# A projection on other PSUM banks, and one table of angles built later

## The chip, the cores and the metric

The kernel runs on one core of one Trainium2 chip. The metric is the device time in microseconds of one execution; lower is better. Three runs of the kernel before gave a median of 1317.6 us (1317.01 to 1318.38). The profile used here is of one further execution, which took 1318.57 us.

The engines named are PE (matrix products), PEld (its weight loads), DVE (the vector engine), ACT (activations and copies), POOL and SP (the queue that issues the large loads). PSUM is the memory that PE writes its products to; here it is cut into eight banks of 128 x 512 numbers.

## The reference

One decoder layer on 256 tokens of width 1024, in float32. The normalised input is multiplied by one wide matrix, and four branches take their parts of the result:

```
proj = h @ w_in
att  = dsa_attention(...)      # indexer relu(q_idx . k_idx), top-64 keys, latent attention
cnv  = short_conv(...)         # gated convolution of width 3
ssm  = s5_mixer(...)           # diagonal complex state space, scan over time, then a gate
mem_o = memory_attention(...)  # 4 heads into 256 memory tokens
merged = sum_r sigmoid(gate_r) * (branch_r @ w_branch[r])
h = layer_norm(alpha * h + merged @ w_o)
h = layer_norm(alpha * h + moe(h))     # 32 experts, top 4 of each token
```

In `s5_mixer` the decay of a state over a step is `exp(lam * dt)`, so the powers of it that a chunked scan needs are sines and cosines of multiples of an angle. `u` is the scan's input, `h @ w_in` in the columns of the state space.

## The kernel before

The program is written as one main stream of projections (`main`, L957 on) and three streams beside it, which are traced a step at a time between the projections: the scan (`scan_all`), the indexer and sparse attention (`sparse_all`) and the memory attention (`memory_all`). After tracing, a scheduler reorders instructions of an engine, except those given to `keep_in_program_order`. Each engine then runs its own list strictly in that order, so an instruction that waits holds up all that stands behind it on its engine.

**Weights.** SP loads each weight matrix in pieces of 1 MB into slabs. A weight is then split into a high and a low part: ACT casts it (L320), DVE subtracts (L325, 128x1024 at a time, two per piece), and PE makes three products of them (L386 to L388). The splits are traced some weights ahead of their use.

**PSUM.** Three pools of banks: `P` with four, `PT` (transposes) with two and `PD` (small products) with two. A product waits until what its bank held before has been read. The projections' results (`pu` for the scan's input, `pmq` for the memory's queries, `pq` for the sparse queries, `pcv` for the convolution) all come from `P`, as do the indexer's scores `prl` (read by ACT's relu, L825) and the latents `pckv` (read by DVE, L1046).

**The scan.** `scan_tables` (L548 on) makes tables of angles. L581 makes the angles within a chunk (`sn`, 128x288), L584 those between chunks (`js`, 128x1024); `wrap` (L569 to L573) brings an angle into the range of the sine. ACT takes the sines (L594 to L597), and DVE goes on (L598 to L651). `scan_in` turns the scan's input round, and `scan_part(m)`, for four quarters m, first builds two matrices on DVE (L679 to L686, eight instructions, of which six of 128x1024), multiplies them on PE (`pkt`, L696/L697, and the transposes `pe`, L707), sends one through DRAM, and then runs the scan itself: `pV` on PE (L719), its copy on ACT (L722), turns by `js` and `jc` on DVE (L660 to L669 and L724 to L730) and the products `py`. `pkt` and `pV` stand in `PD`, as do the logits `pml` of the memory attention (L923), which DVE reduces (L926, L927) and ACT exponentiates (L929).

**After the branches.** Gates (`pg`), branch outputs (`pbr`), the output product and the router follow, and then the experts: a stream of 1 MB loads of their weights which starts when the slabs of the part ahead come free.

Of the kernel before, what the change touches and what calls it, by code (L numbers as in the profile page):

```python
# [17 lines left out]
AF = mybir.ActivationFunctionType  # L18
OP = mybir.AluOpType
# [10 lines left out]
NG, GN, GP = 32, 16, 64  # L30
SC = 8
NJ = T // SC
# [139 lines left out]
def tile_trunk(ctx, tc, a, out):  # L172
    nc = tc.nc
    PE, V, S, G = nc.tensor, nc.vector, nc.scalar, nc.gpsimd
# [16 lines left out]
    def P(nm):  # L191
        return ps.tile([128, 512], FT, name=nm, tag="pp", bufs=4)
# [261 lines left out]
    def small(shape, nm, bufs=2):  # L454
        return keep.tile(shape, FT, name=nm, bufs=bufs)
# [71 lines left out]
    p = PT("pvc")  # L527
# [25 lines left out]
    res = {}  # L553

    def scan_tables():

        L = B(128, 2, NG)
        p = PT("pl")
# [9 lines left out]
        def wrap(t, kt):  # L568
            V.tensor_scalar(kt, t, 1.0 / TWO_PI, MAGIC, op0=OP.mult, op1=OP.add)  # L569
            V.tensor_scalar(kt, kt, MAGIC, None, op0=OP.subtract)  # L570
            for c in (PI_A, PI_B, PI_C):
                V.scalar_tensor_tensor(t, kt, -c, t, op0=OP.mult, op1=OP.add)
            V.tensor_scalar(t, t, PI_IN, -PI_IN, op0=OP.min, op1=OP.max)  # L573
# [3 lines left out]
        kk, jj = B(128, NG * NJ), B(128, NG, NJ)  # L577
        G.iota(jj.ap, pattern=[[0, NG], [1, NJ]], base=0, channel_multiplier=0, allow_small_or_imprecise_dtypes=True)
        wrap(XA.ap[:, 1, :], kk.ap[:, :NG])
        sn, js, jc = sn_, js_, jc_  # L580
        V.tensor_tensor(sn.ap, tau.ap, XA.ap[:, 1:2, :].to_broadcast([128, NT, NG]), op=OP.mult)  # L581
        wrap(sn.ap, kk.ap[:, :NT * NG].rearrange("p (t g) -> p t g", t=NT))
        yield
        V.tensor_tensor(js.ap, jj.ap, sn.ap[:, SC, :].unsqueeze(2).to_broadcast([128, NG, NJ]), op=OP.mult)  # L584
        wrap(js.ap, kk.ap.rearrange("p (g j) -> p g j", g=NG))
        kk.free()
        jj.free()
        yield
        mag, th = mag_, B(128, NG)
        V.tensor_tensor(mag.ap, tau.ap, XA.ap[:, 0:1, :].to_broadcast([128, NT, NG]), op=OP.mult)  # L590
# [2 lines left out]
        sh = B(128, NT, NG)  # L593
        S.activation(sh.ap, sn.ap, AF.Sin, scale=0.5)  # L594
        S.activation(sn.ap, sn.ap, AF.Sin)
        S.activation(jc.ap, js.ap, AF.Sin, scale=0.5)
        S.activation(js.ap, js.ap, AF.Sin)  # L597
        V.tensor_tensor(jc.ap, jc.ap, jc.ap, op=OP.mult)  # L598
        V.tensor_scalar(jc.ap, jc.ap, -2.0, 1.0, op0=OP.mult, op1=OP.add)
        yield  # L600
        V.tensor_tensor(sh.ap, sh.ap, sh.ap, op=OP.mult)
        pr = pr_
        V.tensor_scalar(pr.ap, sh.ap, -2.0, 1.0, op0=OP.mult, op1=OP.add)
# [6 lines left out]
        pi = sn  # L610
# [18 lines left out]
        for i in range(2):  # L629
            p = PT("pc")  # L630
# [18 lines left out]
        pis, npr = pis_, tau  # L649
# [4 lines left out]
        res.update(pr=pr, pi=pi, pis=pis, npr=npr, js=js, jc=jc, mag=mag)  # L654
        yield

    def turn(dst, src, sine, sign):

        lo, hi = slice(0, 64), slice(64, 128)
        V.scalar_tensor_tensor(dst[lo], src[hi], sign, sine[hi], op0=OP.mult, op1=OP.mult)  # L660
        V.scalar_tensor_tensor(dst[hi], src[lo], -sign, sine[lo], op0=OP.mult, op1=OP.mult)

    def scan_part(m):

        pr, pi, pis, npr, js, jc, mag = (res[k].ap for k in ("pr", "pi", "pis", "npr", "js", "jc", "mag"))
        gs = slice(m * 8, m * 8 + 8)
        b1f = bb1.ap.rearrange("p g n -> p (g n)")[:, m * 128:]
        b1, b2, C1, C2 = bb1.ap[:, gs], bb2.ap[:, gs], CC[0].ap[:, gs], CC[1].ap[:, gs]
        tg = lambda t, k: t[:, k:k + SC, gs].rearrange("p t g -> p g t").unsqueeze(3).to_broadcast([128, 8, SC, GN])  # L669
        bg = lambda t: t.unsqueeze(2).to_broadcast([128, 8, SC, GN])  # L670

        blk1, blk2 = B(128, SLAB), B(128, SLAB)
        Cp, tE = carve(blk1, *[(128, 8, SC, GN)] * 2)
        M3 = carve(blk1, (128, 1024), (128, 8, 128))[1]
        kp = carve(blk1, (128, 1024), (128, 2, (2 * SC - 1) * GN))[1]
        E, M1 = carve(blk2, (128, 8, SC, GN), (128, 8, 128))
        Vs, Vr, rt, a8 = carve(blk2, *[(128, 8 * NJ)] * 3, (128, 8, NJ))
        C0, St = res["io2"][1 + m % 2 * 2:3 + m % 2 * 2]
        V.tensor_copy(C0.ap[0:64], C1[0:64])  # L679
        V.tensor_scalar(C0.ap[64:128], C1[64:128], -1.0, None, op0=OP.mult)  # L680
        V.tensor_tensor(Cp.ap, bg(C1), tg(npr, 1), op=OP.mult)
        V.tensor_tensor(tE.ap, bg(C2), tg(pi, 1), op=OP.mult)
        V.tensor_tensor(Cp.ap, Cp.ap, tE.ap, op=OP.subtract)
        V.tensor_tensor(E.ap, bg(b1), tg(pr, 0), op=OP.mult)
        V.tensor_tensor(tE.ap, bg(b2), tg(pis, 0), op=OP.mult)
        V.tensor_tensor(E.ap, E.ap, tE.ap, op=OP.add)  # L686
        yield

# [3 lines left out]
        p = PD("pkt")  # L692
# [11 lines left out]
        for q4 in range(2):  # L704
            p = PT("pe")
# [11 lines left out]
        p = PD("pV")  # L717
# [18 lines left out]
        p = PD("py")  # L736
# [16 lines left out]
    def scan_in():  # L753

        uP = res["uP"]
        W1, U = B(128, 8, SC, GN), res["U"]
        for s4 in range(2):
            p = PT("pus")
            for i in range(4):
                PE.transpose(p[:, i * 128:(i + 1) * 128],  # L760
                             uP.ap[:, SC - 1 - (s4 * 4 + i)].rearrange("p m j -> p (m j)"), ident)
            S.copy(W1.ap[:, :, s4 * 4:s4 * 4 + 4, :].rearrange("p q s n -> p s q n"),
                   p.rearrange("p (s q n) -> p s q n", s=4, q=8))
        for q4 in range(2):
            p = PT("puq")
            for i in range(4):
                PE.transpose(p[:, i * 128:(i + 1) * 128],
                             W1.ap[:, q4 * 4 + i].rearrange("p s n -> p (s n)"), ident)
            S.copy(U.ap[:, q4 * 4:q4 * 4 + 4].rearrange("p q m j -> p (q m j)"), p)
        W1.free()  # L770
        res["Y1"] = res["io2"][0]
        yield
# [180 lines left out]
        res["br3"] = oX  # L953


    def projs(ids, xx, nm, put):
        for c, i in enumerate(ids):  # L957
            p = P(nm)
            for j in range(2):
                w = take(i, j)  # L960
                projT(p[:, j * 256:(j + 1) * 256], w, 0, xx)
                w.done()
            put(c, p)
            yield
# [4 lines left out]
    def main():  # L969
# [6 lines left out]
        for c, i in enumerate(ID_V):  # L976
            w = take(i)
            p = P("pv")
# [25 lines left out]
        p = P("pqi")  # L1004
# [9 lines left out]
        p = P("pki")  # L1014
# [14 lines left out]
        wix = keep.tile([128, 2, IH], FT, name="wix")  # L1029
# [28 lines left out]
        res.update(io_blk=io_blk, U=U, io2=carve(io_blk[1], (128, SC, 8, GN), *[(128, 8, GN), (128, 8, NJ + 1)] * 2))  # L1058
        for c, _ in enumerate(projs(ID_S, hX, "pu", lambda c, p: S.copy(
                uP.ap[:, :, 2 * c:2 * c + 2, :].rearrange("p s m j -> p m j s"),  # L1060
                p.rearrange("p (m j s) -> p m j s", m=2, s=SC)))):
            if c == 0:
                latents()
            yield
# [11 lines left out]
        for c2 in range(2):  # L1076
# [11 lines left out]
            for i in range(2):  # L1088
                c = c2 * 2 + i
                V.tensor_scalar(cv.ap[:, i, :], vv.ap[:, i, 0:T], cw(c, 0), cw(c, 3), op0=OP.mult,  # L1090
                                op1=OP.add)
                for k in (1, 2):
                    V.scalar_tensor_tensor(cv.ap[:, i, :], vv.ap[:, i, k:k + T], cw(c, k), cv.ap[:, i, :],
                                           op0=OP.mult, op1=OP.add)
# [8 lines left out]
        for n, r in enumerate((1, 3, 2, 0)):  # L1103
            if r == 2:
# [3 lines left out]
                for c in range(4):  # L1108
                    w = take(ID_GL, c // 2)
                    p = P("pgl")  # L1110
# [15 lines left out]
            for d2 in range(KC // 2):  # L1126
                p = P("pg")
# [7 lines left out]
                p = P("pbr")  # L1135
# [3 lines left out]
                m = mg.ap[:, 2 * d2:2 * d2 + 2, :].rearrange("p a t -> p (a t)")  # L1139
# [78 lines left out]
    def both(*gens):  # L1218
        live = list(gens)
        while live:  # L1220
            for g in list(live):
                try:
                    next(g)
                except StopIteration:
                    live.remove(g)
            yield

    def scan_all():
        for _ in range(SCAN_AT):
            yield  # L1230
        yield from scan_tables()
        while "uP" not in res:
            yield
        yield from scan_in()
        yield from both(scan_part(0), scan_part(1))
        yield from both(scan_part(2), scan_part(3))
        yield from scan_out()
# [83 lines left out]
    for b in range(2):  # L1321
        mu, r, nm = mv1[:, b, 0:1], r1[:, b:b + 1], nm1[:, b:b + 1]
# [15 lines left out]
        p = PD("prk")  # L1338
# [434 lines left out]
```

## Time and profile before

| | us |
|---|---|
| median of three runs | 1317.6 (1317.01 to 1318.38) |
| the profiled execution | 1318.57 |
| its span (first to last instruction) | 1316.7 |
| PE busy | 1214.9 (92%) |
| DVE busy | 469.8 (36%) |
| ACT busy | 319.6 (24%) |
| mean DMA rate over the span | 352 GB/s |

A group of rows names an engine, a line of the kernel, the operation, the tile written and the tile read. Buffer numbers are left out, so two buffers of one name look alike. The number in brackets at a row's end is how long the engine stood idle ahead of the instruction, and which instruction ended that. The instructions of an engine overlap a little, so that a run of matmuls of 0.28 us each can start every 0.12 us. PEclk is the share of full speed that PE's clock was granted.

### The profile page before, as it was taken

How to read it: one execution, taken by the hardware profiler on the slowest of the kernel's cores; microseconds unless marked ns; L12 is line 12 of the kernel's file. 1: busy time of each engine (PE TensorE's matmuls, PEld its weight loads, DVE VectorE, ACT ScalarE, POOL GpSimd, SP SyncE). 2: the span in 40 equal slices, each digit the busy share in tenths (PEclk: the TensorE clock that was granted, in tenths of full speed). 3: DMA queues.
4: the chain of work that ended last, by engine and by line, in shares of the span. 5: the costliest groups of instructions: out<-in, count | busy, mean ns of one | idle time of the engine just before them, and what ended most of it. 6: DMA issues, size and time to landing. Idle time of an engine off the chain costs nothing. (4 is left out here: it accounts for less than half of the span.)

```text
span 1316.7 us, 17368 instructions
## 1 busy us (share of the span) xinstructions
PE 1214.9 (92%) x6928; PEld 669.2 (51%) x6928; DVE 469.8 (36%) x972; ACT 319.6 (24%) x639; POOL 107.3 (8%) x158
## 2 busy tenths in 40 slices
PE   8799999999999999999999999898989898899984
PEld 8699999889853333333343333333333333333321
DVE  5896976755632133221212213021221212130214
ACT  4735545544422111011211102011010102020101
POOL 1103020246110000000000000000000000000001
PEclk9999999999999999999999999999999999999998
DMA  9816458974889999999999999999999999999993
GB/s 249 273 36 172 130 144 291 292 249 164 319 324 412 419 420 419 419 420 419 420 419 418 420 419 421 420 419 420 419 421 418 420 420 418 421 419 420 412 413 131
DMA packets 115238, 463.38 MB, mean 352 GB/s; under 512 B 19304, under 2 KB 54192, under 8 KB 68016
## 3 DMA queue, kind: packets, MB, share of 16 engines
q1 hardware_dynamic: 112512, 456.37, 87.6%
q0 software_dynamic: 2608, 5.83, 1.7%
q8 instruction: 57, 0.93, 0.3%
q14 instruction: 29, 0.24, 0.0%
q10 hardware_dynamic: 32, 0.01, 0.0%
HBM read 459.09 MB, written 3.08 MB: 351 GB/s over the span
## 5 line engine op out<-in xcount | busy, mean ns | idle before, releaser
L1500 PE MATMUL hp<-slab,slab 128*64 128x512 f32 x2048 | 484.7, 597 | 31.2 <-DMA slab<-in_w_up_dram 30.8
L1500 PEld LDWEIGHTS hp<-slab,slab 128*64 128x64 f32 x2048 | 157.6, 137 | 321.5 <-issue 238.5
L1518 PE MATMUL dp<-slab,slab 128*64 128x512 f32 x1024 | 232.3, 597 | 2.2 <-ACT slab L1515 1.2
L1518 PEld LDWEIGHTS dp<-slab,slab 128*64 128x64 f32 x1024 | 72.4, 137 | 127.3 <-issue 120.9
L325 DVE TENSOR_TENSOR slab<-slab,slab 128x1024 fp32r<-128x1024 f32 (+1 forms) x90 | 110.3, 1235 | 55.8 <-ACT slab L320 50.5
L320 ACT CAST slab<-slab 128x1024 fp32r<-128x1024 f32 x90 | 92.6, 1048 | 78.9 <-DMA slab<-in_w_in_dram 16.5
L1391 ACT ACTIVATE slab<-pxs,pcol 128x128 f32<-128x128 f32 x128 | 48.0, 457 | 235.2 <-PE pxs L1386 225.1
L1491 DVE CAST slab<-id 128x64 fp32r<-128x64 f32 x34 | 5.1, 192 | 221.3 <-PE hp L1494 212.5
L1377 POOL TENSOR_SCALAR slab<-slot_i,slot 128x64 f32<-128x64 f32 x32 | 13.9, 453 | 803.6 <-PE pta L1513 701.6
L388 PE MATMUL pg<-slab,slab 128*128 128x256 f32 x256 | 74.4, 291 | 0.0
L386 PE MATMUL pg<-slab,slab 128*128 128x256 f32 x256 | 74.3, 290 | 0.0
L387 PE MATMUL pg<-slab,slab 128*128 128x256 f32 x256 | 73.6, 288 | 0.0
L1386 PEld LDWEIGHTS pxs<-slab,slab 128*128 128x128 f32 x512 | 59.7, 192 | 25.7 <-issue 23.5
L1457 ACT CAST slab<-psg 128x256 fp32r<-128x256 f32 x16 | 6.0, 372 | 255.5 <-PE psg L1455 255.5
L1386 PE MATMUL pxs<-slab,slab 128*128 128x128 f32 x512 | 65.9, 282 | 1.1 <-DVE slab L1377 0.7
L1443 DVE TENSOR_SCALAR slab<-hp 128x256 f32<-128x256 f32 x64 | 27.0, 422 | 76.5 <-PE pta L1513 76.5
L1534 DVE TENSOR_TENSOR slab<-slab,psc 128x512 f32<-128x512 f32 x60 | 38.6, 684 | 43.7 <-PE psc L1530 43.7
L386 PEld LDWEIGHTS pg<-slab,slab 128*128 128x128 f32 x256 | 49.8, 194 | 2.0 <-issue 1.5
L388 PEld LDWEIGHTS pg<-slab,slab 128*128 128x128 f32 x256 | 49.9, 195 | 1.1 <-issue 1.1
L387 PEld LDWEIGHTS pg<-slab,slab 128*128 128x128 f32 x256 | 49.8, 194 | 0.3 <-issue 0.2
L1513 PE MATMUL pta<-ident,slab 128*128 128x128 f32 x128 | 26.5, 290 | 24.2 <-ACT slab L1515 24.0
L1515 ACT COPY slab<-pta 128x256 f32<-128x256 f32 x64 | 23.9, 375 | 94.3 <-PE pta L1513 94.3
(446 smaller groups left out, 1533.8 us busy)
## 6 DMA issues: line engine op xcount, KB each, us to landing
slab<-in_w_up_dram SPq DMA_DIRECT2D x256, 1024.0 KB, 19.9
slab<-in_w_down_dram SPq DMA_DIRECT2D x126, 1024.0 KB, 19.9
slab<-in_w_in_dram SPq DMA_DIRECT2D x29, 1024.0 KB, 6.6
slab<-in_w_branch_dram SPq DMA_DIRECT2D x8, 1024.0 KB, 7.3
slab<-in_w_mem_kv_dram SPq DMA_DIRECT2D x4, 1024.0 KB, 10.9
slab<-in_w_o_dram SPq DMA_DIRECT2D x4, 1024.0 KB, 8.1
slab<-kp_d POOLq DMA_DIRECT2D x32, 64.0 KB, 3.9
slab<-in_w_down_dram SPq DMA_DIRECT2D x4, 512.0 KB, 16.6
```

The costliest lines, as they stand in the source:

```text
L320: ins = S.copy(r_(hi[:, sl]), src[:, sl])
L325: ins = eng.tensor_tensor(r_(lo[:, p0:p1]), src[:, p0:p1], hi[:, p0:p1], op=OP.subtract)
L386: PE.matmul(dst, lh, rh, start=first, stop=False)
L387: PE.matmul(dst, lh, rl, start=False, stop=False)
L388: PE.matmul(dst, ll, rh, start=False, stop=last)
L1386: PE.matmul(p[:, i * 128:(i + 1) * 128], hN.ap[:, b, k * 128:(k + 1) * 128], self.S2.ap[:, b].rearrange("p e s -> p (e s)"), start=b == 0 ...
L1391: S.activation(self.xs.ap[:, k, :], p[:, i * 128:(i + 1) * 128], AF.Identity, bias=col(3, k), scale=col(2, k))
L1443: V.tensor_scalar(l.ap, hv[:, :, :, 1], LIMIT, -LIMIT, op0=OP.min, op1=OP.max)
L1500: PE.matmul(hp[nb][e * 64:(e + 1) * 64, :], xs[:, k, e * CAP:(e + 1) * CAP], w, start=start, stop=k == KC - 1, skip_group_check=True)
L1513: PE.transpose(p[:, j * 128:(j + 1) * 128], l.ap[:, j, :], ident)
L1518: PE.matmul(dp[nb][e * 64:(e + 1) * 64, :], aT.ap[:, k, e * 64:(e + 1) * 64], w, start=k == 0, stop=k == KC - 1, skip_group_check=True)
L1534: V.tensor_tensor(y, y, p, op=OP.add)
```

## The change

1. `projs` takes the pool of banks as an argument, and the scan's input is projected with `PD` in place of `P`.
2. The angles between chunks leave `scan_tables`: their product, their wrap, their two sines and the two instructions that make the cosine move into a new stream `turns`, traced after `scan_in`. A copy of 128x32 (`step8`) keeps the angles they are made from.
3. `scan_tables` now waits, while it is traced, until the indexer's weights `wix` are there, before the instructions after the sines.
4. For the first two quarters of the scan, six of the eight instructions that build the two matrices are given to `keep_in_program_order`.

```diff
--- before.py
+++ after.py
@@ -580,11 +580,8 @@
         sn, js, jc = sn_, js_, jc_
         V.tensor_tensor(sn.ap, tau.ap, XA.ap[:, 1:2, :].to_broadcast([128, NT, NG]), op=OP.mult)
         wrap(sn.ap, kk.ap[:, :NT * NG].rearrange("p (t g) -> p t g", t=NT))
-        yield
-        V.tensor_tensor(js.ap, jj.ap, sn.ap[:, SC, :].unsqueeze(2).to_broadcast([128, NG, NJ]), op=OP.mult)
-        wrap(js.ap, kk.ap.rearrange("p (g j) -> p g j", g=NG))
-        kk.free()
-        jj.free()
+        step8 = small([128, NG], "step8", 1)
+        V.tensor_copy(step8, sn.ap[:, SC, :])
         yield
         mag, th = mag_, B(128, NG)
         V.tensor_tensor(mag.ap, tau.ap, XA.ap[:, 0:1, :].to_broadcast([128, NT, NG]), op=OP.mult)
@@ -593,11 +590,9 @@
         sh = B(128, NT, NG)
         S.activation(sh.ap, sn.ap, AF.Sin, scale=0.5)
         S.activation(sn.ap, sn.ap, AF.Sin)
-        S.activation(jc.ap, js.ap, AF.Sin, scale=0.5)
-        S.activation(js.ap, js.ap, AF.Sin)
-        V.tensor_tensor(jc.ap, jc.ap, jc.ap, op=OP.mult)
-        V.tensor_scalar(jc.ap, jc.ap, -2.0, 1.0, op0=OP.mult, op1=OP.add)
         yield
+        while "wix" not in res:
+            yield
         V.tensor_tensor(sh.ap, sh.ap, sh.ap, op=OP.mult)
         pr = pr_
         V.tensor_scalar(pr.ap, sh.ap, -2.0, 1.0, op0=OP.mult, op1=OP.add)
@@ -654,6 +649,19 @@
         res.update(pr=pr, pi=pi, pis=pis, npr=npr, js=js, jc=jc, mag=mag)
         yield
 
+        def turns():
+
+            V.tensor_tensor(js.ap, jj.ap, step8.unsqueeze(2).to_broadcast([128, NG, NJ]), op=OP.mult)
+            wrap(js.ap, kk.ap.rearrange("p (g j) -> p g j", g=NG))
+            kk.free()
+            jj.free()
+            yield
+            S.activation(jc.ap, js.ap, AF.Sin, scale=0.5)
+            S.activation(js.ap, js.ap, AF.Sin)
+            V.tensor_tensor(jc.ap, jc.ap, jc.ap, op=OP.mult)
+            V.tensor_scalar(jc.ap, jc.ap, -2.0, 1.0, op0=OP.mult, op1=OP.add)
+        res["turns"] = turns
+
     def turn(dst, src, sine, sign):
 
         lo, hi = slice(0, 64), slice(64, 128)
@@ -676,13 +684,15 @@
         E, M1 = carve(blk2, (128, 8, SC, GN), (128, 8, 128))
         Vs, Vr, rt, a8 = carve(blk2, *[(128, 8 * NJ)] * 3, (128, 8, NJ))
         C0, St = res["io2"][1 + m % 2 * 2:3 + m % 2 * 2]
-        V.tensor_copy(C0.ap[0:64], C1[0:64])
-        V.tensor_scalar(C0.ap[64:128], C1[64:128], -1.0, None, op0=OP.mult)
-        V.tensor_tensor(Cp.ap, bg(C1), tg(npr, 1), op=OP.mult)
-        V.tensor_tensor(tE.ap, bg(C2), tg(pi, 1), op=OP.mult)
+
+        hold = tc.keep_in_program_order if m < 2 else lambda ins: ins
+        hold(V.tensor_copy(C0.ap[0:64], C1[0:64]))
+        hold(V.tensor_scalar(C0.ap[64:128], C1[64:128], -1.0, None, op0=OP.mult))
+        hold(V.tensor_tensor(Cp.ap, bg(C1), tg(npr, 1), op=OP.mult))
+        hold(V.tensor_tensor(tE.ap, bg(C2), tg(pi, 1), op=OP.mult))
         V.tensor_tensor(Cp.ap, Cp.ap, tE.ap, op=OP.subtract)
-        V.tensor_tensor(E.ap, bg(b1), tg(pr, 0), op=OP.mult)
-        V.tensor_tensor(tE.ap, bg(b2), tg(pis, 0), op=OP.mult)
+        hold(V.tensor_tensor(E.ap, bg(b1), tg(pr, 0), op=OP.mult))
+        hold(V.tensor_tensor(tE.ap, bg(b2), tg(pis, 0), op=OP.mult))
         V.tensor_tensor(E.ap, E.ap, tE.ap, op=OP.add)
         yield
 
@@ -953,9 +963,9 @@
         res["br3"] = oX
 
 
-    def projs(ids, xx, nm, put):
+    def projs(ids, xx, nm, put, bank=P):
         for c, i in enumerate(ids):
-            p = P(nm)
+            p = bank(nm)
             for j in range(2):
                 w = take(i, j)
                 projT(p[:, j * 256:(j + 1) * 256], w, 0, xx)
@@ -1058,7 +1068,7 @@
         res.update(io_blk=io_blk, U=U, io2=carve(io_blk[1], (128, SC, 8, GN), *[(128, 8, GN), (128, 8, NJ + 1)] * 2))
         for c, _ in enumerate(projs(ID_S, hX, "pu", lambda c, p: S.copy(
                 uP.ap[:, :, 2 * c:2 * c + 2, :].rearrange("p s m j -> p m j s"),
-                p.rearrange("p (m j s) -> p m j s", m=2, s=SC)))):
+                p.rearrange("p (m j s) -> p m j s", m=2, s=SC)), PD)):
             if c == 0:
                 latents()
             yield
@@ -1232,6 +1242,7 @@
         while "uP" not in res:
             yield
         yield from scan_in()
+        yield from res["turns"]()
         yield from both(scan_part(0), scan_part(1))
         yield from both(scan_part(2), scan_part(3))
         yield from scan_out()
```

In the built programs the counts on the engines stay as they are but for one more DVE instruction (the copy) and one more load of an activation table on ACT. The instructions below carry the number of the slab that they use.

On ACT, from the scan's tables to the relu of the second pair of indexer scores (`prl`). Before, with the sines of the angles between chunks at L596 and L597:

```order
L1037 COPY wix<-pckv 128x8
L1038 ACTIVATE slab_608,ss<-pckv 128x128
L596 ACTIVATE slab_121<-slab_121 128x1024
L1037 COPY wix<-pckv 128x8
L1038 ACTIVATE slab_608,ss<-pckv 128x128
L597 ACTIVATE slab_121<-slab_121 128x1024
L1039 ACT_TABLE_LOAD
L1039 ACTIVATE rr<-ss,eps_t 128x2
L634 COPY slab_123<-pc 128x512 x2
L825 ACTIVATE slab_124<-prl 128x128
```

After (the lines have other numbers there: the same sines are L659 and L660, the relu is L835):

```order
L1049 ACT_TABLE_LOAD
L1049 ACTIVATE rr<-ss,eps_t 128x2
L629 COPY slab_123<-pc 128x512 x2
L835 ACTIVATE slab_124<-prl 128x128
L835 ACTIVATE slab_683<-prl 128x128
L835 ACTIVATE slab_124<-prl 128x128
L835 ACTIVATE slab_683<-prl 128x128
L320 CAST slab_927<-slab_517 128x1024
L659 ACT_TABLE_LOAD
L659 ACTIVATE slab_121<-slab_121 128x1024
L1069 COPY slab_694<-pu 128x64x8
L1062 COPY slab_612<-pct 128x256
```

The first sine stands behind the first four relus and a table load of its own, and no longer ahead of them; the second stands later still.

On PE, where the first query projection `pq` ends, with the scan's first products `pkt` and `pe` and the memory's logits `pml`. Before, the end of the second `pkt`, then `pe`, `pml` and the second `pq`:

```order
L696 MATMUL pkt<-slab_704,slab_122 32x16
L697 MATMUL pkt<-slab_1001,slab_122 32x112
L696 MATMUL pkt<-slab_704,slab_122 32x16
L697 MATMUL pkt<-slab_1001,slab_122 32x112
L707 MATMUL pe<-ident,slab_1002 128x128 x8
L923 MATMUL pml<-slab_198,slab_124 128x256 x4
L386 MATMUL pq<-slab_196,slab_1018 128x256
L387 MATMUL pq<-slab_197,slab_1018 128x256
```

After, the end of the first `pq`, then `pml` and the second `pq`:

```order
L386 MATMUL pq<-slab_196,slab_927 128x256
L387 MATMUL pq<-slab_197,slab_927 128x256
L388 MATMUL pq<-slab_196,slab_928 128x256
L933 MATMUL pml<-slab_198,slab_527 128x256 x4
L386 MATMUL pq<-slab_196,slab_996 128x256
L387 MATMUL pq<-slab_197,slab_996 128x256
L388 MATMUL pq<-slab_196,slab_997 128x256
```

And after, where the second `pq` (48 matmuls) ends:

```order
L386 MATMUL pq<-slab_196,slab_996 128x256
L387 MATMUL pq<-slab_197,slab_996 128x256
L388 MATMUL pq<-slab_196,slab_997 128x256
L706 MATMUL pkt<-slab_695,slab_122 32x16
L707 MATMUL pkt<-slab_1057,slab_122 32x112
L706 MATMUL pkt<-slab_695,slab_122 32x16
```

The two pairs `pkt` and `pe` came ahead of `pml` and now come behind it and behind the second `pq`. All three of `pml`, its twin and `pkt` write banks of `PD`, so `pkt` now waits until the exponentials of `pml` are read out; the built program's first `pkt` waits for the second exponential.

On DVE, ahead of the reduction of `pml` (L926 before, L936 after; L686 and L696 are the last instruction of a quarter's matrices, MAX and MATCH_REPLACE are the rounds of the indexer's top-k). Before, the end of the second quarter's matrices:

```order
L685 TENSOR_TENSOR slab_1001<-slab_123,slab_122 128x1024
L840 MAX m_1011<-slab_608 128x8
L686 TENSOR_TENSOR slab_1002<-slab_1002,slab_1001 128x1024
L841 MATCH_REPLACE slab_608<-m_1011,slab_608 128x128
L325 TENSOR_TENSOR slab_1019<-slab_517,slab_1018 128x1024
L840 MAX m_1014<-slab_608 128x8
L325 TENSOR_TENSOR slab_1019<-slab_517,slab_1018 128x1024
L841 MATCH_REPLACE slab_608<-m_1014,slab_608 128x128
L325 TENSOR_TENSOR slab_1191<-slab_1073,slab_1190 128x1024
L840 MAX m_1157<-slab_608 128x8
```

After, the same place:

```order
L695 TENSOR_TENSOR slab_1067<-slab_123,slab_122 128x1024
L851 MATCH_REPLACE slab_527<-m_1077,slab_527 128x128
L696 TENSOR_TENSOR slab_1068<-slab_1068,slab_1067 128x1024
L850 MAX m_1080<-slab_527 128x8
L936 TENSOR_REDUCE mx<-pml 128x2
L851 MATCH_REPLACE slab_527<-m_1080,slab_527 128x128
L937 TENSOR_SCALAR mx<-mx 128x2
L936 TENSOR_REDUCE mx<-pml 128x2
L325 TENSOR_TENSOR slab_1111<-slab_1051,slab_1110 128x1024
```

The reduction stood 20 rows behind the second quarter's L686; it now stands two rows behind it, and ahead of that L686 stand two more splits of a weight and more of the rounds.

## Rows read from the trace of the kernel before

**Rows 1.** The profile page: slices of a fortieth of the span, 32.9 us each
```profile
DVE  5896976755632133221212213021221212130214
...
DMA  9816458974889999999999999999999999999993
GB/s 249 273 36 172 130 144 291 292 249 164 319 324 412 419 420 419 419 420 419 420 419 418 420 419 421 420 419 420 419 421 418 420 420 418 421 419 420 412 413 131
```

**Rows 2.** PE's waits, 55 to 200 us: in total, times, longest
```profile
PE pu L386 <- ACT slab L825: 7.1, 1, 7.1
PE pe L707 <- DVE slab L686: 1.4, 1, 1.4
```

**Rows 3.** PE's timeline, 57 to 75 us: start, duration, line, operation, [idle before]
```profile
57.88 0.71 PE L820 MATMUL prl<-slab 32*128 32x128 f32 x8
65.72 0.58 PE L386 MATMUL pu<-slab,slab 128*128 128x256 f32 x1 [7.13 <-ACT slab L825]
...
69.29 0.28 PE L387 MATMUL pu<-slab,slab 128*128 128x256 f32 x1
```

**Rows 4.** ACT's timeline, 60 to 66 us
```profile
60.43 1.06 ACT L596 ACTIVATE slab<-slab 128x1024 f32<-128x1024 f32 x1 [3.64 <-DVE slab L573]
...
62.78 1.28 ACT L1039 ACT_TABLE_LOAD   x1
...
65.21 0.79 ACT L825 ACTIVATE slab<-prl 128x128 f32<-128x128 f32 x4
```

**Rows 5.** DVE's timeline, 52 to 75 us
```profile
52.09 1.23 DVE L584 TENSOR_TENSOR slab<-slab,slab 128x1024 f32<-128x1024 f32 x1
...
74.27 1.23 DVE L325 TENSOR_TENSOR slab<-slab,slab 128x1024 fp32r<-128x1024 f32 x1 [0.82 <-ACT slab L320]
```

**Rows 6.** Windows: length, busy time of five engines, PEclk, DMA share, GB/s
```profile
66.00:68.00 2.00, 2.00 (x10) 2.00 (x11) 2.00 (x5) 0.00 (x1) 0.00 (x0) 0.50 0.00 0
168.00:170.00 2.00, 2.00 (x12) 2.00 (x12) 2.00 (x5) 1.19 (x2) 0.27 (x1) 0.56 0.35 54
120.00:178.00 58.00, 55.83 (x523) 52.01 (x522) 56.84 (x108) 28.64 (x56) 9.93 (x22) 0.97 0.44 125
```

**Rows 7.** DVE's timeline, 92 to 105 us
```profile
92.99 1.21 DVE L686 TENSOR_TENSOR slab<-slab,slab 128x1024 f32<-128x1024 f32 x1
...
94.38 1.22 DVE L325 TENSOR_TENSOR slab<-slab,slab 128x1024 fp32r<-128x1024 f32 x1
...
100.36 0.28 DVE L841 MATCH_REPLACE8 slab<-m,slab 128x128 f32<-128x128 f32 x1
...
103.68 0.69 DVE L926 TENSOR_REDUCE mx<-pml 128x2 f32<-128x512 f32 x1 [0.57 <-PE pml L923]
```

**Rows 8.** ACT's timeline, 104 to 108 us
```profile
104.65 1.28 ACT L929 ACT_TABLE_LOAD   x1 [1.20 <-DVE mx L927]
105.95 0.47 ACT L929 ACTIVATE slab<-pml,mx 128x256 f32<-128x256 f32 x1
...
106.77 0.20 ACT L929 ACTIVATION_READ_ACCUMULATOR slab<-pml,mx 128x1 f32 x1
```

**Rows 9.** PE's timeline, 99 to 113 us
```profile
102.61 1.89 PE L923 MATMUL pml<-slab,slab 128*128 128x256 f32 x8
104.15 0.47 PE L386 MATMUL pq<-slab,slab 128*128 128x256 f32 x1
...
110.09 1.87 PE L719 MATMUL pV<-slab,slab 128*128 128x32 f32 x16
...
112.62 0.36 PE L386 MATMUL pcv<-slab,slab 128*128 128x256 f32 x1
```

**Rows 10.** ACT's timeline, 119 to 121 us
```profile
119.52 0.36 ACT L722 COPY slab<-pV 128x256 f32<-128x256 f32 x1
```

**Rows 11.** DVE's timeline, 120 to 180 us
```profile
120.89 0.42 DVE L660 SCALAR_TENSOR_TENSOR slab<-slab,slab 64x256 f32<-64x256 f32 x1
...
177.35 1.23 DVE L325 TENSOR_TENSOR slab<-slab,slab 128x1024 fp32r<-128x1024 f32 x1
```

## Prediction

> **What bounds the kernel now.** I read the page's slices first. From the thirteenth on, about 395 us into the span, the core moves 412 to 421 GB/s and its DMA share is 9 almost to the end: the experts are bound by their weight loads [rows 1]. Ahead of that the rates go up and down between 36 and 324 GB/s, so the first 360 us or so are bound by the engines. The experts' loads follow the slabs that this part frees, so what it gains or loses moves the end one for one.
>
> Second, the waits of PE. Between 55 and 200 us two matter: 7.1 us of the scan's input `pu` for ACT's relu, and 1.4 us of a transpose `pe` for DVE [rows 2]. On the timeline PE ends the indexer's scores at 58.59 (57.88 + 0.71) and starts `pu` at 65.72 [rows 3].
>
> Third, why the relu is late. ACT stands idle 3.64 us until DVE has wrapped the angles between chunks, then takes two sines, loads a table for 1.28 us, and reaches the relu only at 65.21 [rows 4]. `pu` does not use what the relu writes: it needs one of the four banks of its pool, all held by scores and latents.
>
> Fourth, the clock. After the wait PE runs at 0.50 of its speed, the 1.2 GHz level [rows 6]: 16 matmuls take 3.57 us, from 65.72 to 69.29 [rows 3]. At the full level, 2.4 GHz, 48 take 5.94 us, from 104.15 to 110.09, or 0.124 each [rows 9].
>
> Last, DVE. From 120 to 178 us it is busy 56.84 of 58 us, and PE 55.83 [rows 6]: there PE has little slack against DVE, and a lead on PE alone need not pass through.
>
> **Other banks for `pu`.** Nothing writes the two banks of the small products between the start of the program and the memory's logits, so `pu` can start right after the scores, at about 59.0 (I add 0.4 to 58.59, since a copy on ACT that PE needs ahead of it now stands behind two sines). That takes away 7.13 - 0.4 = 6.7 us of waiting and 3.57 - 16 x 0.124 = 1.6 us of slow clock, 8.3 us in all. The second `pu` has a bank of its own and waits for nothing new.
>
> **The angles between chunks.** On DVE nothing is taken away: their product and wrap still stand at the same place in its list, from 52.09 on [rows 5], and one small copy is added (0.2 us). On ACT the sines move behind the first four relus, with a table load of their own. These relus write a buffer that DVE's tables use before; from 52.1 I count 27 instructions of DVE up to the last of those, seven of 128x1024 (four at about 1.14 from start to start, three at 0.6) and twenty small ones of 0.1 to 0.6, by estimate 11.3 us in all, so they start at about 63.5. Then a cast, the load (1.28, as in [rows 4]), the sine (1.06), two copies and a cast precede the second four relus, which I place at 70.1. DVE waits about 2.1 us for them, where it waited 0.8 us at 74.27 [rows 5].
>
> ScalarE: Activation LUTs, a page of the Trainium skill, counts about 2.7 us for each switch of tables (Table sets: the hidden batching unit), though its section on what the load costs has 1283 ns. By the larger figure the added load would take 1.4 us more, push DVE back by as much and leave 0.4 us of the gain below. Both loads shown took 1.28 us [rows 4, 8], so the trace bears out the smaller one.
>
> **A new wait on PE.** This is the price. With `pu` early the memory's queries are early too, and the memory's logits `pml` now stand ahead of the scan's `pkt` on PE. They share two banks, so `pkt` waits until ACT has taken the exponentials of `pml`, and these wait for the reduction on DVE, which stands behind the matrices of the scan's second quarter. Before, those end at 92.99 + 1.21 = 94.2 [rows 7]. Ahead of them now stand eight subtractions L325 where six stood, two more at about 1.14 from start to start (1.22 each in [rows 7]), 2.3 us; two and a half more top-k rounds at about 0.47 (a replacement alone is 0.28), 1.2 us; and 1.3 us more of waiting for the relus: 94.2 + 4.8 = 99.0. Then the reduction (0.69) and its small follower with a round between, 1.3 us; the load of the table of exponentials, 1.28; and the first two exponentials, half of 105.95 to 107.7, 0.9 [rows 8]. So `pkt` starts at 102.5.
>
> PE is there earlier. The first query projection ended at about 99.3 before (`pkt` and `pe`, 3.3 us, stand between it and `pml` at 102.61 [rows 9]); 8.3 earlier, that is 91.0. Then `pml`, 1.54 (102.61 to 104.15), and the second projection, 5.94: 98.5. The new wait is 102.5 - 98.5 = 4.0 us, and 0.7 us more go to ACT's copy of `pe`, for which the second `pe` waits now that no projection covers it. The bounds are 0, if DVE gets there 4 us earlier than I count, and 7, if the relus or splits hold it up once more as long. I take 4.0, the sum of the rows.
>
> Queued behind the waiting `pkt` are `pe`, the second pair, the transposes of the memory attention and the first convolution product, which started at 112.62 before, after 1.7 us of `pV` [rows 9] that now come later.
>
> **The clock again.** The wait of 7.13 us was followed by half speed, and so was the wait of 1.4 us with small matmuls on both sides: 0.56 in 168 to 170 [rows 6]. The new one lies between the two, so I count the same 1.6 us for it. The bounds are 0 and 3, since the transposes behind the wait may run slowly as well.
>
> **Behind it.** ACT's copies of `pV`, which start the scan's steps on DVE, now stand behind one more convolution product and two casts, at about 123.7 where the first was at 119.52 [rows 10]; so DVE begins its full stretch at about 124.1 instead of 120.89 [rows 11], 3.2 us late, with about 3.1 us less in it (two subtractions and two steps of the indexer are done already). It ended at 177.35 + 1.23 [rows 11] and ends at the same time give or take 1 us. PE meets it in a better order: a gate product of 48 matmuls, 5.9 us, now stands ahead of `pkt` and `pe` of the third quarter. It covers the old wait of 1.4 us, but by DVE's order the fourth quarter's `pe` then waits about 2.2 us and a branch product about 1.4. With what the better order saves I count 0.2 us lost; the bounds are -2 and +4.
>
> **Sum.** 8.3 - 4.0 - 0.7 - 1.6 - 0.2 = 1.8 us. On the profiled execution's 1318.57 that gives 1316.8; the median of the three runs is 0.97 below that execution, so the forecast is 1315.8. A measurement of this kernel can tell from no change what differs by over 0.2%, 2.6 us.
>
> **Rivals.**
> - The wait at `pkt` is short. For it: the 4.8 us by which DVE comes later are a sum of three small terms, and the waiting for the relus rests on my placing of ACT's list. Against: DVE is at 9 tenths in the third slice, 66 to 99 us [rows 1], so there are no gaps that the two subtractions could fall into. Then 8.3 - 0.7 - 0.2 = 7.4 us stay: 1310.2.
> - DVE absorbs everything: PE, whatever its lead at 120, waits for a stretch on DVE that ends when it ended before. For it: 56.84 of 58 us [rows 6]. Against: the gate product that PE can do meanwhile. Then 1317.5.
> - Slower. ACT's copies of `pV` come so late that DVE's full stretch ends later. From the point where they let DVE begin 3.1 us after 120.89, at 124.0, the price is one for one, and I put that at 124.1. If PE's clock stays low from the new wait through part of the next two convolution products (32 matmuls, 3.2 us more), DVE begins at 127.3 and ends 3.3 us later; PE's lead ahead of it is then spent in waits, and the time is 1317.6 + 3.3 = 1320.9.
> - The banks are not free after all and `pu` waits as before: 1317.6. The order on PE speaks against it.
>
> **How the numbers follow.** Forecast 0.43 (own range 1314 to 1317, a third of it below 1315.0), short wait 0.25, DVE absorbs it 0.12, slower 0.18, banks 0.02. Faster by over 0.2%: 0.25 + 0.43/3 = 0.40 (rounded up). Within: 0.28 + 0.12 + 0.02 = 0.42. Slower: 0.18. The range is 1309.5 to 1320: it leaves out about a third of the short wait (its own spread reaches 1308.5) and half of the slow case.
>
> **What the changed profile would show.** `pu` starts within 1 us of the scores' end at PEclk 1.00, and the wait for the relu is gone. A wait of `pkt` of 2.5 to 5 us for ACT's exponential stands at about 98, with half clock behind it. DVE's second L696 ends at 98 to 100. The first step of the scan on DVE after `pV` starts at 123 to 126, and DVE is full until 177 to 180. The forecast is wrong if `pkt` does not wait, if PE waits over 6 us in all between 120 and 200, or if the experts' first loads move by less than half of PE's lead at 190.

## The result, and the profile after

The changed kernel takes 1332.5 us (median of 4, 1330.9 to 1333.0) beside 1317.7 for the kernel before: a ratio of 1.0108 [1.0096, 1.012], 14.7 us slower. The forecast was 1315.8, with 1320 at the top of its range: wrong in sign and size. In the profiled executions the span grows by 12.4 us, from 1316.7 to 1329.1.

The page's slices say where. From the thirteenth slice on the core again moves 406 to 422 GB/s, as in [rows 1]; the clock dips in the sixth slice, 166 to 199 us, and in the ninth, 266 to 299 us, a place that the prediction never looked at.

```profile
DVE  5895985745642123311213112120311212121314
...
PEclk9999989989999999999999999999999999999997
...
GB/s 257 260 64 142 128 173 279 229 222 182 224 312 406 420 421 421 421 421 421 422 421 419 421 421 421 421 421 421 421 421 422 421 420 421 422 421 421 413 413 137
```

Up to 105 us the steps came as forecast. PE's waits from 55 to 200 us, in answer to [rows 2] (waiter, releaser, total, times, longest):

```profile
PE pkt L706 <- ACT slab L939: 3.1, 1, 3.1
PE pe L717 <- DVE slab L696: 2.2, 1, 2.2
PE pkh L867 <- ACT slab L868: 1.1, 1, 1.1
```

PE's timeline after, in answer to [rows 3, 9]:

```profile
58.01 0.71 PE L830 MATMUL prl<-slab,slab 32*128 32x128 f32 x8
58.65 0.39 PE L386 MATMUL pu<-slab,slab 128*128 128x256 f32 x1
...
90.91 1.89 PE L933 MATMUL pml<-slab,slab 128*128 128x256 f32 x8
...
101.60 0.27 PE L706 MATMUL pkt<-slab,slab 128*32 128x16 f32 x7 [3.05 <-ACT slab L939]
```

`pu` follows the scores at once, 7.1 us earlier than in [rows 3], and PE keeps the full clock there. The price of it stands where it was expected: `pkt` waits 3.05 us for the exponentials of `pml`. ACT's timeline, in answer to [rows 4, 8]:

```profile
63.28 0.79 ACT L835 ACTIVATE slab<-prl 128x128 f32<-128x128 f32 x4 [2.10 <-DVE rr L1054]
...
65.00 1.28 ACT L659 ACT_TABLE_LOAD   x1
...
69.39 0.78 ACT L835 ACTIVATE slab<-prl 128x128 f32<-128x128 f32 x4
```

DVE's timeline, in answer to [rows 5, 7, 11]:

```profile
69.70 0.35 DVE L844 SCALAR_TENSOR_TENSOR slab<-slab,wix,slab 128x128 f32<-128x128 f32 x1 [1.99 <-ACT slab L835]
...
96.81 1.22 DVE L696 TENSOR_TENSOR slab<-slab,slab 128x1024 f32<-128x1024 f32 x1
...
126.39 0.42 DVE L668 SCALAR_TENSOR_TENSOR slab<-slab,slab 64x256 f32<-64x256 f32 x1
```

The relus start at 63.28 and 69.39 and DVE waits 1.99 us for them. The second L696 ends at 98.03. But the scan's first step on DVE (L668) starts at 126.39, not 124.1.

The windows after (columns: stretch, length, busy time and count of PE, PEld, DVE, ACT, POOL, PEclk, DMA share, GB/s), the first two in answer to [rows 6]:

```profile
120.00:178.00 58.00, 54.73 (x507) 51.41 (x505) 52.45 (x101) 25.94 (x50) 8.40 (x19) 0.94 0.40 113
160.00:180.00 20.00, 17.38 (x162) 15.91 (x161) 19.61 (x28) 6.82 (x13) 5.46 (x11) 0.78 0.26 65
...
260.00:264.00 4.00, 1.41 (x8) 0.81 (x8) 3.96 (x7) 1.64 (x3) 1.99 (x2) 0.92 0.69 250
264.00:274.00 10.00, 9.83 (x20) 5.39 (x21) 4.17 (x8) 2.23 (x4) 0.00 (x0) 0.50 0.64 214
274.00:280.00 6.00, 6.00 (x41) 6.00 (x40) 1.62 (x3) 2.75 (x10) 0.00 (x0) 0.75 0.01 3
```

PE's lead over the kernel before, taken at the same piece of work, is 7.1 us at `pu` and 3.6 at the late `pml` (126.85, before 130.43). By 191 us, after the same number of matmuls, it is 1.3 us behind, and at the end of the branch product (258.4, before 254.1) 4.3; one wait on the way is 2.18 us of `pol` for ACT at 240.32. Most of the rest goes between there and 280. PE's timeline before, around the scan's output (its transposes `pyt`), the attention's logits `pal` and weights `pat`, and the gate product `pgl`, which reads the scan's result:

```profile
231.91 1.04 PE L782 MATMUL pyt<-ident,slab 128*128 128x128 f32 x8
...
244.28 1.14 PE L870 MATMUL pal<-slab 64*128 64x256 f32 x8
...
254.08 0.28 PE L386 MATMUL pgl<-slab,slab 128*128 128x256 f32 x1
...
255.31 0.70 PE L890 MATMUL pat<-ident,slab 128*128 128x128 f32 x4 [0.71 <-DVE slab L884]
...
257.68 1.99 PE L895 MATMUL pol<-slab,slab 128*128 128x512 f32 x4
...
265.32 0.39 PE L386 MATMUL pg<-slab,slab 128*128 128x256 f32 x1
```

The same stretch after:

```profile
247.63 1.03 PE L792 MATMUL pyt<-ident,slab 128*128 128x128 f32 x8
248.60 1.14 PE L880 MATMUL pal<-slab 64*128 64x256 f32 x8
...
258.27 0.28 PE L388 MATMUL pbr<-slab,slab 128*128 128x256 f32 x1
261.95 0.41 PE L900 MATMUL pat<-ident,slab 128*128 128x128 f32 x2 [3.40 <-DVE slab L894]
...
264.17 3.78 PE L905 MATMUL pol<-slab,slab 128*128 128x512 f32 x4 [0.59 <-ACT slab L901]
...
273.04 0.58 PE L387 MATMUL pgl<-slab,slab 128*128 128x256 f32 x1
...
280.16 0.28 PE L386 MATMUL pg<-slab,slab 128*128 128x256 f32 x1
```

And DVE after:

```profile
250.94 2.29 DVE L796 SCALAR_TENSOR_TENSOR slab<-slab,pcol,pyt 128x128 f32<-128x128 f32 x8
253.07 1.40 DVE L884 TENSOR_TENSOR slab<-pal,slab 128x256 f32<-128x256 f32 x4
...
260.43 2.63 DVE L894 TENSOR_SCALAR slab<-slab,asm 128x256 f32<-128x256 f32 x4
...
266.77 1.23 DVE L379 TENSOR_TENSOR slab<-slab,slab 128x1024 fp32r<-128x1024 f32 x1 [1.11 <-ACT slab L378]
```

`pyt` comes 15.7 us later: it now stands behind one more gate and branch product. So the scan's last eight steps on DVE (L796) stand right ahead of the softmax (L884), and the softmax's last step (L894) ends at 263. Before, `pgl` filled that time, since what it reads was ready at 249.2, as DVE's timeline before shows:

```profile
247.99 1.23 DVE L379 TENSOR_TENSOR slab<-slab,slab 128x1024 fp32r<-128x1024 f32 x1
```

Now that is ready at 268.0 (L379), PE has nothing else, and it waits 3.40 us for `pat`. Then it runs at the 1.2 GHz level, 0.50 from 264 to 274 and 0.75 on the mean to 280: `pol` takes 3.78 us where it took 1.99. From the end of the branch product to the next `pg` it is 254.1 to 265.3 before and 258.4 to 280.2 after, 10.6 us more. The waits are 4.2 us (3.40 + 0.23 + 0.59) where 0.95 stood before (0.71 + 0.24), so 3.3 more, and the clock costs about 6.5 (half of 10, a quarter of 6); about 0.8 is left unexplained.

What shifted it is one line of the diff, `yield from res["turns"]()`. The new stream holds a `yield`. The scan's stream and the main one are traced in turns, so each `yield` sets everything of the scan behind it one step of the main stream later: `pkt`, the four quarters, the output.

The experts' first load is issued at 291.15, before at 274.25: 16.9 us later, though the span grows by 12.4 only. The last section comes back to this.

### The profile page after: what moved, and what is told of

It is laid out like the page before. It is cut to its first block, busy times and chain, and to the rows that moved or that the text cites. A ratio compares the mean times of both kernels' runs of the same rounds, so it can differ in the third digit from the quotient of the medians.

```text
span 1329.1 us, 17368 instructions
## 1 busy us (share of the span) xinstructions
PE 1229.3 (92%) x6928; PEld 679.2 (51%) x6928; DVE 472.9 (36%) x973; ACT 321.0 (24%) x640; POOL 106.5 (8%) x158
## 6 DMA issues: line engine op xcount, KB each, us to landing
slab<-in_w_mem_kv_dram SPq DMA_DIRECT2D x4, 1024.0 KB, 10.7
```

## The experiments

Theory S: this one empty step of tracing costs the time, and the rest of the change brings a gain. The first rivals: A, the moved angles and tables cost it; B, the early input projection itself does, by the waits that it sets off. D, formed after the second run: DVE is the bound, and what comes early on PE ends in waits. Each run has its own comparison with the kernel before.

**The banks alone.** The kernel before with the banks of `pu` and nothing else:

```diff
-    def projs(ids, xx, nm, put):
+    def projs(ids, xx, nm, put, bank=P):
...
-            p = P(nm)
+            p = bank(nm)
...
-                p.rearrange("p (m j s) -> p m j s", m=2, s=SC)))):
+                p.rearrange("p (m j s) -> p m j s", m=2, s=SC)), PD)):
```

> The kernel before with the first edit alone: the scan's input is projected on the two other banks. Theory S (the extra tracing step that the new stream puts into the scan moves the scan's last products behind one more gate product, and that costs some 11 us near 260 us): this kernel has no extra step, so it is 6 to 9 us faster than before, 1308.5 to 1311.5. Theory B (the early scan input itself does the harm, by what it brings forward): slower than before, over 1320. Theory A (the sines moved on ACT, their table load and the kept order do it): as S here.

Measured 1316.0, ratio 0.9984 [0.9975, 0.9994]: faster, but by 2.2 us (3.3 by spans), well short of S and of A, which had said the same. B falls: the early `pu` does not cost. Its waits and windows:

```profile
PE pct L1051 <- DVE slab L1046: 3.3, 2, 2.9
```

```profile
60.00:80.00 20.00, 16.67 (x127) 15.96 (x126) 19.86 (x44) 10.62 (x22) 0.15 (x2) 0.91 0.17 53
80.00:100.00 20.00, 19.95 (x218) 19.05 (x218) 19.86 (x42) 10.02 (x17) 1.76 (x5) 1.00 0.16 50
```

PE now waits for DVE at the latents' transposes instead, and DVE is busy 39.7 of 40 us. PE's lead of 7 shrinks to 3.1 at `pkt`.

**No extra step.** The changed kernel with the new stream run through without giving way:

```diff
-        yield from res["turns"]()
+        for _ in res["turns"]():
+            pass
```

> The changed kernel whole, but the new stream is traced through at once, without a step of its own, so that the scan's later parts are traced at the steps where they were before. Theory S: the loss goes and the gain of the early scan input stays, 1308 to 1312. Theory B: slower than before, over 1320, since the scan input is as early as in the changed kernel. Theory A: about 1332, since sines, table load and kept order stay.

Measured 1321.7, 1.0028 [1.0016, 1.0039]. This is 3.5 us slower than before, so the step costs 11.2 of the 14.7 us. A's 1332 falls, but so does S's gain; B's "over 1320" comes out here, though B had fallen in the run above. PE leads by 6.7 us at `pkt` (92.62, before 99.29), and loses it at 119.8. Three rows in order: SP's wait for a slab, ACT's wait for the load that SP issued late, PE's for ACT:

```profile
SPq L269 <- DVE m L850: 24.8, 1, 24.8
```

```profile
ACT slab L320 <- DMA slab<-in_w_in_dram: 10.4, 2, 7.6
```

```profile
119.80 2.07 PE L955 MATMUL pmo<-slab,slab 128*128 128x256 f32 x4 [3.86 <-ACT slab L732]
```

Read together: DVE's top-k (L850) frees a slab late, so a weight load starts late, ACT's casts wait, and behind them its copy of `pV`. This chain is read from rows and was not tested. SP's wait alone does not tell the kernels apart: it waits 18.4 us for the top-k in the kernel before and 21.9 with the banks alone, where no cast of ACT waits for a load between 100 and 130.

**The step given back later.** The changed kernel, with its last two quarters and the output one step earlier:

```diff
-        yield from both(scan_part(2), scan_part(3))
+        late = both(scan_part(2), scan_part(3))
+        next(late)
+        yield from late
```

> The changed kernel with its extra step ahead of the first two quarters of the scan, and one step taken out ahead of the third and fourth, so that only the first half of the scan is late. Theory S: the 11 us near 260 us are back and the wait of pkt for the exponential stays at about 3 us: 1317 to 1322. Theory B and theory A: within 3 us of the changed kernel's 1332.5.

Measured 1323.8, 1.0045 [1.0028, 1.0062]: 5.5 us slower than before, 1.8 above S's range. So 9.2 of the 14.7 us are back, though `pkt` still waits 3.06; B and A fall. `pyt` starts at 240.49, `pat` waits 1.30, and the clock is 1.00 from 260 to 280. So most of the loss comes with the late half of the scan and the output, as S has it.

**The step alone.** The kernel before with one bare `yield` between `scan_in()` and the quarters, nothing else changed:

> The kernel before with nothing but one more empty step in the scan's stream, between its input and its first two quarters. Theory S: 8 to 15 us slower than before, 1326 to 1333, with PE waiting near 260 us for the softmax and the scan's output, and half clock behind that. Theory B and theory A: within 2 us of before.

Measured 1336.9, 1.0157 [1.0136, 1.0179]: 18.7 us for a line that computes nothing, more than S said; A and B have no way to explain it. At 266.72 `pat` waits 3.41 us for the softmax, with the clock at 0.50 from 268 to 274, where S had placed it. But PE is 9.1 us behind already at the end of the branch product in front of it (263.2, before 254.1), so this place is less than half of the price here.

**The step ahead of the last two quarters.** The kernel before with the `yield` between the two `both(...)` lines:

> The kernel before with one empty step in the scan's stream ahead of its third and fourth quarters only, so that the first half keeps its place. Theory S (the late output of the scan, near 260 us, is most of the step's price): 8 to 13 us slower than before, 1326 to 1331. Its rival, that the price is paid in the first half, near 100 to 140 us: within 4 us of before, under 1322.

Measured 1333.6, 1.012 [1.0103, 1.0137], 15.5 us, above S's range by 2.6.

**The step ahead of the output alone.** The kernel before with the `yield` ahead of `scan_out()`. O puts most of the cost here, Q in the quarters:

> The kernel before with one empty step ahead of the scan's output alone (the transposes pyt and the steps to the gated product pgl); all four quarters keep their places. Theory O (the late output costs most: its DVE instructions fall ahead of a softmax that PE waits for, the product pgl waits for the output, and half clock follows): 7 to 10 us slower than before, 1325 to 1328. Theory Q (the late third and fourth quarters cost most, by what stands behind them from 160 to 245 us): under 1321.

Measured 1328.3, 1.0083 [1.0066, 1.01]: 10.7 us. PE's waits from 230 to 300 us and its window:

```profile
PE pol L895 <- ACT slab L891: 5.7, 3, 4.3
PE pat L890 <- DVE slab L884: 3.6, 2, 3.4
```

```profile
262.00:268.00 6.00, 5.01 (x10) 2.32 (x10) 4.50 (x7) 2.12 (x3) 0.00 (x0) 0.50 0.65 230
```

The same wait of 3.4 us and half clock, without any other edit: the late output is most of the loss, as O has it (the time is 0.3 above its range), and Q falls. Not all of the 10.7 us are lost at this place. At the end of the branch product PE is 3.9 us behind already (258.0, before 254.1), after a wait of `pol` of 4.3 us at 237, where before `pyt` and a gate product stood; from there to the next `pg` it takes 18.5 us, before 11.2, so 7.3 more. The three runs nest, so, if the costs add, by differences of the medians the late third and fourth quarter cost 15.5 - 10.7 = 4.8, and the first two with `pkt` 18.7 - 15.5 = 3.2.

One rival was not tried apart: the output also gives back the scan's slabs, so a late output lets weight loads start late. After, SP waits 3.8 us for `pyt` and 1.8 for L796 between 190 and 295, before 1.6 and nothing. No wait of PE from 200 to 300 names a load.

**The latents later.** With S's gain missing, D against P, by which PE's own order (the latents' transposes ahead of the second `pu`) takes it. The banks alone, with `latents()` behind the second `pu`:

```diff
-            if c == 0:
+            if c == 1:
                 latents()
```

> The first edit alone, and the latents traced behind the second scan input instead of the first, so that PE's second scan input no longer stands behind a transpose that waits 3.3 us for DVE. Theory D (from 60 to 178 us the real bound is DVE, and a lead of PE alone is not kept): no better than the banks alone by over 1.5 us, 1313.5 to 1317. Theory P (the wait behind the first scan input is what kept the banks alone from their 8 us): 1309 to 1312.

Measured 1314.9, 0.9975 [0.9966, 0.9985]: as D has it, and P falls. By their distances from the kernel before it is 1.0 us faster than the banks alone, and the two intervals overlap.

**No step, and no fixed order.** As the second run, with `hold` doing nothing:

```diff
-        hold = tc.keep_in_program_order if m < 2 else lambda ins: ins
+        hold = lambda ins: ins
```

> The changed kernel without the extra step and without the kept order of the scan's first matrices. Theory D: small instructions of these matrices move ahead into DVE's wait for the second relus, so DVE loses less there, 1316 to 1320. Theory A (late sines and their table load cost the 5.7 us that the kernel without the step loses on the banks alone, whatever DVE does meanwhile): 1320 to 1323.

Measured 1320.4, 1.0015 [1.0005, 1.0024], on the edge between both: it settles nothing.

**No step, no fixed order, no wait for `wix`.** As the last run, and the two lines `while "wix" not in res: yield` are left out. W: this wait, which traces the tables behind the splits, costs what is left:

> The changed kernel without the extra step, the kept order and the tracing wait for the indexer's weights: of the four edits the banks and the later sines stay. Theory D: within 1.5 us of the kernel that leaves out the step and the kept order, since the wait moves nothing that DVE is late with. Theory W (the wait delays the tables and so DVE's whole list): 2 us or more faster than that.

Measured 1318.0, 1.0003 [0.9992, 1.0013], 2.3 us less than the run above by the medians, as W has it, but the two intervals overlap. With the banks alone at 1316.0, the moved angles and tables bring no gain in the time of any run.

**The latents later, the late half of the scan earlier.** The run with the latents later, with the edit of the step given back. If a step later costs, does a step earlier gain?

> The banks, the latents behind the second scan input, and the scan's third and fourth quarters one step earlier than before. Theory S, turned round (the earlier the scan's end, the better): 2 to 5 us faster than the banks with later latents, 1310 to 1313. Theory D (DVE is full from 60 to 178 us, and work moved into it must push other work out): 1315 to 1320.

Measured 1317.2, 1.0001 [0.9991, 1.001]: no gain, and some 2.8 us worse than without this edit, as D has it; S turned round misses. PE waits 2.6 us for `pkh` and 2.7 for `pol`.

**The latents later, the scan's tables earlier.** The run with the latents later, with the scan's stream started after one step of the main one:

```diff
-SCAN_AT = 2
+SCAN_AT = 1
```

> The banks, the latents behind the second scan input, and the whole scan stream started one tracing step earlier. The order on PE stays nearly as in the kernel without that shift. Theory D: within 2 us of it, 1313 to 1317. Theory S, turned round: 2 us or more faster, under 1313.

Measured 1308.7, 0.9938 [0.9921, 0.9955]: 8.9 us faster than before, and the fastest of all. D missed. S turned round has its number, but not by its path: behind its tables the stream waits until the scan's input is there (`while "uP" not in res`), so only the tables moved. The product of the angles (L584) starts at 36.07 us, before at 52.09, while `pkt` and `pyt` stand behind the same products as before. Its windows, and those of before for the first two stretches:

```profile
30.00:40.00 10.00, 9.99 (x83) 9.58 (x82) 8.95 (x21) 7.57 (x16) 3.36 (x2) 1.00 1.08 324
40.00:50.00 10.00, 9.54 (x53) 7.91 (x53) 10.00 (x16) 8.23 (x12) 0.86 (x3) 1.00 1.09 347
90.00:100.00 10.00, 10.00 (x131) 9.15 (x130) 7.49 (x22) 6.69 (x16) 1.82 (x5) 1.00 0.57 166
```

```profile
30.00:40.00 10.00, 9.46 (x73) 8.60 (x73) 4.65 (x11) 5.89 (x12) 3.13 (x2) 1.00 1.06 325
40.00:50.00 10.00, 9.01 (x58) 7.14 (x60) 7.50 (x17) 8.96 (x14) 0.00 (x0) 1.00 1.09 348
```

DVE does 6.8 us more between 30 and 50 us, where it had room, and is no longer full at 90 to 100. PE leads by 8.0 us at `pkt` (91.30) and by 7.7 at the end of the convolution products (153.48, before 161.19), and the lead lasts. So D had the bound right but not that it could be moved.

## Why the prediction was wrong

- **Other banks for `pu`: right here.** `pu` starts 0.35 us earlier than forecast (58.65 for 59.0), and the first query projection ends at 90.91 for 91.0. That 8.3 us of lead is worth 8.3 us of time was wrong: alone the banks give 2.2. DVE was read as the bound from 120 us on [rows 6]; a rival had it at 9 tenths from 66 to 99, but the lead was not set against that. In the kernel before it is busy 38.7 of the 40 us from 60 to 100, and with the banks alone the lead on PE there is spent in waits for it:

```profile
60.00:80.00 20.00, 14.28 (x107) 13.99 (x108) 18.73 (x41) 9.42 (x21) 0.00 (x0) 0.83 0.03 4
80.00:100.00 20.00, 19.95 (x194) 19.44 (x192) 19.97 (x37) 8.55 (x12) 0.67 (x3) 1.00 0.24 77
```

- **The angles: right in their times.** Relus at 63.28 and 69.39 for 63.5 and 70.1, DVE's wait 1.99 for 2.1. The added load took 1.28 us, from 65.00, right behind a cast that ends at 64.99 and right ahead of the sine at 66.29. That is the 1283 ns that the Trainium skill, ScalarE: Activation LUTs (What ACT_TABLE_LOAD costs), gives for the load; the drain of about 1380 ns by which that section comes to 2.66 us for a switch does not show here. But the edits beside the banks lose 2 to 6 us on the banks alone even without the step (1318.0 to 1321.7, beside 1316.0), and no term counted that.
- **The new wait at `pkt`: right in mechanism.** 3.05 us for 4.0; L696 ended at 98.03 for 99.0. The granted clock behind it was 0.74 from 102 to 104 and 0.70 from 104 to 108, 1.7 us in all, for the 1.6 counted. At the late `pml` the lead is 3.6 us where the terms up to there leave 2.0.
- **Behind it: the step that failed.** It put 0.2 us (-2 to +4) on all that follows, and looked at PE and DVE up to 190 us only. The fourth quarter's `pe` wait came as forecast (2.15 for 2.2). But the lead fell from 3.6 to -1.3 by 191, 4.9 us lost, with the clock at 0.78 from 160 to 180 (before 0.91). And nothing at all was counted behind that, where 3.0 us more go up to the end of the branch product and 10.6 from there to 280. The prediction saw that a gate product now stands ahead of `pkt` of the third quarter, and called this the better order; it did not ask what else the same shift moves. `pyt` and `pgl` were in no step. With the late output alone the kernel before loses 10.7 us, 7.3 of them at this same place; that 10.7 is so near the 10.6 here is chance.
- **The rivals.** The slower one named the late copies of `pV`. DVE did start late, at 126.39 for 124.1, which by that rival's own count from 124.0 is a price of 2.4 us. It may be a part of the 4.9 us lost by 191, but the larger loss lies behind that stretch. The sign of PE waiting over 6 us between 120 and 200 did not come. The last sign measures the move of the experts' first loads by PE's lead at 190; there was no such lead, and the first load came 16.9 us later.

Open: how much of the 3.5 us left without the step is the wait for `wix` and how much the fixed order (single differences of 1.3 and 2.3 us, intervals overlapping), and why the step costs 18.7 us in the kernel before and 11.2 in the changed one. With the step both issue the experts' first load at the same time (290.98 in the run of the step alone, 291.15 after); without it they do so at 274.25 and 280.17. So what the other edits lose ahead of the experts is not lost a second time with the step; which wait hides it was not tried apart.

## What to carry to other kernels

Where streams are traced in turns, an added `yield` is an edit of every later part of its stream: follow each of these to its last consumer, here the product that reads the scan's result, and price the gap that it used to fill. A later wait of the stream for another's result can take up a shift, as with SCAN_AT, which moved the tables alone. Before counting a lead on one engine, look at how full the next one is in that same stretch; here the lead lasted only when DVE's work, too, moved into its own idle time (30 to 50 us, 0.9938 of the time before). A step of tracing is also cheap to vary: with the banks moved and the latents later (0.9975), the one number SCAN_AT brought 5.7 us more.

## What was not expected of the hardware

One wait of PE of 3.40 us was followed by about 13 us at half clock: 0.50 from 264 to 274, with PE busy 9.83 of the 10 us, back at full only at 277. The wait cost 3.4 us and the clock about 6.5. In the kernel before, 7.13 us of waiting were followed by 3.57 us of slow matmuls [rows 3], and the 3.05 us at `pkt` by 0.74 from 102 to 104 and 0.70 from 104 to 108. So the length of a wait did not tell what the clock behind it costs; behind this one stood `pat`, `pol` and `pal`, behind the first the 48-matmul products of the scan's input. Which difference decides was not tried.

The experts' loads run a little faster in every kernel with the moved angles. From the issue of the first one to the end, the five kernels that have them (after, no extra step, step given back, and the two runs without the fixed order) take 1038.0 to 1039.2 us, the eight others 1041.3 to 1042.7; their rate from 620 to 820 us is 421 GB/s against 419 or 420. So the changed kernel wins back about 3 us of what it loses ahead of the experts, which "one for one" in the prediction leaves out. The fixed order and the wait for `wix` are not what does it, since the run without both has it too; the cause is open.
